# Weight loads on GpSimd's queue, and GpSimd's arithmetic shared out between ScalarE and VectorE, in a two-layer hybrid trunk

## The chip, the cores and the metric

The kernel runs on one core of one Trainium2 chip. The metric is the device time of one execution in microseconds (us), from the first to the last instruction of that core with what the device adds around them; lower is better.

## What is computed

The reference is a two-layer trunk over 768 tokens: 256 context tokens and 512 latent ones, 1024 channels each, all in float32. Each layer is a token-mixing part and a convolutional feed-forward part, both between RMS norms whose result is scaled and shifted by values made from a conditioning vector:

```python
hl = modulate(rmsnorm(xl, norm_g[l, 0]), sh1_l, sc1_l)        # the same for the context, hc
z  = split_columns(hl @ p['w_in'])                             # 6912 columns
ya = s5_branch(...)                 # diagonal state-space scan, both directions, then a GLU
yb = latent_window_attention(...)   # rotary, window of 128, sink logits
yc = hgrn2_branch(...)              # chunked gated linear recurrence, both directions
xl = xl + g1_l * rmsnorm(merge_branches(ya, yb, yc, gates, w_branch, w_out), norm_g[l, 1])
hl = modulate(rmsnorm(xl, norm_g[l, 2]), sh2_l, sc2_l)
xl = xl + g2_l * rmsnorm((silu(a) * g) @ w_down, norm_g[l, 3])  # a, g = conv(hl @ w_up)
```

The second layer does not make the context stream any further, and the latent stream is the output.

## The kernel before

**Products.** Every large product (`w_in`, `w_branch`, `w_glu`, `w_out`, `w_up`, `w_down`) runs on TensorE in a rounded 32-bit format, with each operand split into a high part and a low rest, so that a block of 128 input channels takes three matmuls: high times high, high times rest, rest times high. `wload` (line 286) brings one weight tile of 128x1024 (512 KB) into `wr`, of which there are three buffers. ScalarE writes its high part `wh`, VectorE the rest `wl = wr - wh`; with that subtraction the `wr` buffer is free, and the next load into it may start. `hold` (line 335) does the same for the down projection. The activations are split in the same way: in a norm (`norm_part`, line 552) TensorE transposes a normalized block into PSUM (`pa`), ScalarE writes h from it with scale and shift, GpSimd copies h into the rounded format (hh, the high part), and VectorE subtracts: hl = h - hh. A norm group is eight such blocks.

**Queues.** Every transfer, the 288 weight loads included, is issued by SyncE (SP), which works through its instructions in order: a load that waits for its buffer holds up all that stands behind it. GpSimd issues none. It computes the hh of the norms, the product with the sine in the rotary step (`att_in`, line 1026), the factor k of the recurrence (`hg_in`, line 1259), a few zero fills (lines 1682 and 1805), and the row of factors `mz` that a scan of the state-space branch runs with (from line 1789).

**Order.** A scheduler sets each engine's order from the program, priorities and its own estimate of durations; weight loads and their splitting have a raised priority. Work of other stages is woven in as filler: `mods_rows` (line 418) makes the modulation values of later stages with multiply-and-sum operations on VectorE (`mscr`, `macc`), on rows loaded from `in_wmodt`, and these stand between the operations of the recurrence.

**Names.** Nearly all rows carry line 121, a helper that records each operation, so one goes by the tiles: `slot` is any of 52 general SBUF buffers, `mm` and `mc` are PSUM tiles of products (512 and 256 tokens), `pa` and `pb` PSUM tiles for the rest, `yd` and `gd` branch results and gates kept in DRAM, `kd`, `tod` and `mt` tables of the state-space branch that are prepared in DRAM, `u` packed inputs of that branch in `ud`.

Of the kernel before, what the change touches and what calls it, by code (L numbers as in the profile page):

```python
# [12 lines left out]
ALU = mybir.AluOpType  # L13
# [113 lines left out]
class Trunk:  # L127
# [158 lines left out]
    def wload(self, src, n=1024):  # L286

        nc = self.nc
        raw = self.t(self.wp, [P, 1024], "wr", F32, bufs=WR)
        wh = self.t(self.wp, [P, 1024], "wh", F32R, bufs=WHB)  # L290
        wl = self.t(self.wp, [P, 1024], "wl", F32R, bufs=WHB)
        with self.tc.high_priority(offset=self.whp):
            nc.sync.dma_start(raw[:, :n], src)
            nc.scalar.activation(wh[:, :n], raw[:, :n], AF.Copy)
            with ExitStack() as ctx:
                if self.gate is not None:
                    ctx.enter_context(self.tc.issue_after(self.gate))
                nc.vector.tensor_sub(wl[:, :n], raw[:, :n], wh[:, :n].bitcast(F32))
        return wh, wl
# [35 lines left out]
    def hold(self, srcs, n):  # L335
# [3 lines left out]
        for m, src in enumerate(srcs):  # L339
# [4 lines left out]
            with self.tc.high_priority(offset=self.whp):  # L344
                nc.sync.dma_start(raw[:, :P * n], src)
                a = n * m
                while a < n * (m + 1):
                    i = a // 6
                    b = min(6 * i + 6, n * (m + 1))
                    r = raw[:, P * (a - n * m):P * (b - n * m)]  # L350
                    c = slice(P * (a - 6 * i), P * (b - 6 * i))
                    nc.scalar.activation(hi[i][:, c], r, AF.Copy)
                    nc.vector.tensor_sub(lo[i][:, c], r, hi[i][:, c].bitcast(F32))
                    a = b
# [197 lines left out]
    def norm_part(self, l, which, xr, tiles, ks, hs):  # L552
# [8 lines left out]
        for k0 in range(0, len(ks), per):  # L561
# [5 lines left out]
            for i, k in enumerate(ks[k0:k0 + per]):  # L567
                if k not in hs:
                    hs[k] = (self.s3(F32R), self.s3(F32R))
                hh, hl = hs[k]  # L570
                h = self.s3()
                nc.scalar.activation(h[:, tk], pt[:, n * i:n * i + n], AF.Identity,
                                     bias=self.mod[l][:, 8 * sh + k, tt:tt + 1],
                                     scale=self.amod[l][:, j, k, tt:tt + 1])
                nc.gpsimd.tensor_scalar(hh[:, tk], h[:, tk], 1.0, 0.0, ALU.mult, ALU.add)
                nc.vector.tensor_sub(hl[:, tk], h[:, tk], hh[:, tk].bitcast(F32))
# [441 lines left out]
    def att_in(self, l, h, t0, out):  # L1018
# [7 lines left out]
        def rope(ps, a):  # L1026
# [3 lines left out]
            nc.vector.stream_shuffle(s[:, 256:], z[:, 256:], swap)  # L1030
            nc.gpsimd.tensor_mul(s[:, 256:], s[:, 256:], sin)
            nc.vector.tensor_mul(z[:, 256:], z[:, 256:], cos)
# [198 lines left out]
    def hg_in(self, l, h, hh, t0, out):  # L1231
# [21 lines left out]
        for d, mt in enumerate((mf, mb)):  # L1253
# [4 lines left out]
            k, qf, f = self.s3(), self.s3(), self.w3()  # L1258
            nc.gpsimd.tensor_scalar(k, th, self.hgn[:, c:c + 1], self.hgc[:, c:c + 1], ALU.mult, ALU.add)
            nc.vector.tensor_scalar(f, th, self.hgb[:, c:c + 1], self.hga[:, c:c + 1], ALU.mult, ALU.add)  # L1260
# [394 lines left out]
    def s5_prep(self, l, space, per, slot):  # L1655
# [6 lines left out]
        for o in range(4):  # L1662
# [18 lines left out]
            b3 = bb.rearrange("p (d k) -> p d k", d=2)  # L1681
            nc.gpsimd.memset(bb, 0.0)
            nc.sync.dma_start(b3[:, :, 0:128], bd[:, :, 128 * o:128 * o + 128])
# [31 lines left out]
    def s5(self, l, ud, t0, res):  # L1715
# [41 lines left out]
        def stage_a(o, d, u2, la):  # L1757
# [33 lines left out]
            m3 = mz.rearrange("p (q c) -> p q c", c=96)  # L1791
            nc.gpsimd.memset(mz, 1.0)
            nc.gpsimd.tensor_mul(m3, m3, m8k[:, x0:x0 + 4].unsqueeze(2).to_broadcast([P, 4, 96]))
            nc.gpsimd.memset(m3[:, :, 0:1], 0.0)
            v.tensor_tensor_scan(xr, mz, za, 0.0, ALU.mult, ALU.add)
# [8 lines left out]
            st = 0 if d == 0 else 31  # L1804
            nc.gpsimd.memset(hcat.rearrange("p (g c) -> p g c", c=96)[:, :, st:st + 1], 0.0)
            for g2 in range(2):
# [225 lines left out]
```

## Time and profile before

| | us |
|---|---|
| median of three runs | 2694.89 (2693.42 to 2697.78) |
| the profiled execution, device time | 2701.07 |
| its span, first to last instruction | 2699.3 |
| TensorE busy | 2536.5 (94% of the span) |
| TensorE weight loads, beside the matmuls | 2129.6 (79%) |
| VectorE busy | 1896.8 (70%) |
| ScalarE busy | 1021.7 (38%) |
| GpSimd busy | 121.0 (4%) |

Row forms used below: a timeline row gives start, duration, engine (SPq is SyncE issuing transfers), operation, output and inputs, count, and in brackets how long the engine was idle before it and what ended that. A windows row gives a stretch, its length, the busy time of PE, PEld, DVE, ACT and POOL with instruction counts, the share of TensorE's full clock that was granted, the DMA share and GB/s. A granted clock near 0.5 is the lower of TensorE's two levels, 1.2 GHz; near 1.0 it is 2.4 GHz.

### The profile page before, as it was taken

How to read it: one execution, taken by the hardware profiler on the slowest of the kernel's cores; microseconds unless marked ns; L12 is line 12 of the kernel's file. 1: busy time of each engine (PE TensorE's matmuls, PEld its weight loads, DVE VectorE, ACT ScalarE, POOL GpSimd, SP SyncE). 2: the span in 40 equal slices, each digit the busy share in tenths (PEclk: the TensorE clock that was granted, in tenths of full speed). 3: DMA queues.
4: the chain of work that ended last, by engine and by line, in shares of the span. 5: the costliest groups of instructions: out<-in, count | busy, mean ns of one | idle time of the engine just before them, and what ended most of it. 6: DMA issues, size and time to landing. Idle time of an engine off the chain costs nothing. (4 is left out here: it accounts for less than half of the span.)

```text
span 2699.3 us, 47069 instructions
## 1 busy us (share of the span) xinstructions
PE 2536.5 (94%) x18436; PEld 2129.6 (79%) x18436; DVE 1896.8 (70%) x4304; ACT 1021.7 (38%) x1813; POOL 121.0 (4%) x182
## 2 busy tenths in 40 slices
PE   5999998899989999999999989899999989999998
PEld 3876776687878898887888878667787778888887
DVE  6799483778576659999974566754767856666656
ACT  3356522221223345442433463562222334443334
POOL 1100000001000010000000011000000000100000
PEclk8999999999989999999999999999999989999999
DMA  7443545453566344534434557422334565333332
GB/s 246 129 127 118 166 146 164 156 165 99 169 210 213 119 128 145 162 108 131 123 102 123 155 180 222 130 82 93 107 116 131 170 213 167 110 121 112 96 100 96
DMA packets 243214, 381.36 MB, mean 141 GB/s; under 512 B 54032, under 2 KB 139440, under 8 KB 242992
## 3 DMA queue, kind: packets, MB, share of 16 engines
q1 hardware_dynamic: 242992, 378.36, 44.8%
q8 instruction: 145, 2.38, 0.4%
q14 instruction: 77, 0.63, 0.1%
HBM read 301.26 MB, written 81.21 MB: 142 GB/s over the span
## 5 line engine op out<-in xcount | busy, mean ns | idle before, releaser
L121 PE MATMUL mm<-slot,wh 128*128 128x512 f32 (+1 forms) x3798 | 1200.3, 394 | 23.5 <-DVE slot L121 9.4
L121 PEld LDWEIGHTS mm<-slot,wh 128*128 128x128 f32 x3798 | 699.8, 190 | 160.9 <-DVE slot L121 13.4
L121 PE MATMUL mm<-slot,wl 128*128 128x512 f32 (+1 forms) x1899 | 742.3, 391 | 2.7 <-issue 1.9
L121 DVE TENSOR_TENSOR slot<-slot,slot 128x384 f32<-128x384 f32 (+17 forms) x1340 | 666.3, 535 | 101.5 <-ACT slot L121 59.3
L121 PE MATMUL mc<-slot,wh 128*128 128x256 f32 (+1 forms) x3082 | 666.7, 309 | 9.4 <-ACT slot L121 7.3
L121 PEld LDWEIGHTS mc<-slot,wh 128*128 128x128 f32 x3082 | 518.8, 193 | 57.2 <-ACT slot L121 10.8
L121 DVE TENSOR_TENSOR wl<-wr,wh 128x1024 fp32r<-128x1024 f32 (+1 forms) x274 | 333.8, 1219 | 239.3 <-ACT wh L121 235.1
L121 ACT ACTIVATE wh<-wr 128x1024 fp32r<-128x1024 f32 (+1 forms) x274 | 288.5, 1053 | 531.3 <-PE mc L121 373.0
L121 PE MATMUL mc<-slot,wl 128*128 128x256 f32 (+1 forms) x1541 | 474.6, 308 | 0.0
L121 PEld LDWEIGHTS mm<-slot,wl 128*128 128x128 f32 x1899 | 359.9, 190 | 72.8 <-DVE wl L121 1.6
L121 PEld LDWEIGHTS pa<-slot,slot 128*32 128x32 f32 (+2 forms) x5696 | 213.2, 133 | 126.5 <-issue 62.3
L121 PE MATMUL pa<-slot,slot 128*32 128x32 f32 (+8 forms) x5696 | 254.8, 227 | 57.8 <-DVE slot L121 26.5
L121 PEld LDWEIGHTS mc<-slot,wl 128*128 128x128 f32 x1541 | 296.7, 193 | 14.1 <-issue 1.2
L121 ACT ACTIVATE slot<-slot 128x768 fp32r<-128x768 f32 (+5 forms) x253 | 168.3, 669 | 367.8 <-DVE slot L121 307.7
L121 ACT ACTIVATE slot<-mm 128x512 f32<-128x512 f32 (+1 forms) x180 | 103.6, 576 | 320.7 <-PE mm L121 299.5
L121 DVE CUSTOM_DVE_ANT_0 mscr<-slot,slot 128x768 bf16<-128x768 f32 (+1 forms) x256 | 178.2, 696 | 41.0 <-DMA slot<-in_wmodt 37.5
L121 ACT ACTIVATE slot<-pa 128x512 f32<-128x512 f32 (+7 forms) x250 | 115.3, 493 | 231.0 <-PE pa L121 189.8
L121 PE MATMUL pa<-cst,slot 128*128 128x128 f32 x900 | 139.5, 286 | 23.8 <-DVE slot L121 13.2
L121 PEld LDWEIGHTS pa<-cst,slot 128*128 128x128 f32 x900 | 107.4, 145 | 53.2 <-ACT slot L121 23.4
L121 PE MATMUL mm<-slot,slot 128*128 128x256 f32 (+1 forms) x784 | 111.1, 319 | 17.4 <-DMA slot<-in_wmod 15.6
L121 DVE SCALAR_TENSOR_TENSOR slot<-slot,slot 128x256 f32<-128x256 f32 (+7 forms) x129 | 92.3, 722 | 41.0 <-ACT slot L121 40.3
L121 PEld LDWEIGHTS mm<-slot,slot 128*128 128x128 f32 (+1 forms) x784 | 93.1, 185 | 22.6 <-issue 17.9
(160 smaller groups left out, 1521.9 us busy)
## 6 DMA issues: line engine op xcount, KB each, us to landing
wr<-in_win SPq DMA_DIRECT2D x108, 512.0 KB
wr<-in_wup SPq DMA_DIRECT2D x88, 512.0 KB
slot<-in_wmodt SPq DMA_DIRECT2D x80, 384.0 KB
wr<-in_wdn SPq DMA_DIRECT2D x32, 512.0 KB
slot<-cad SPq DMA_DIRECT2D x48, 256.0 KB
wr<-in_wbr SPq DMA_DIRECT2D x24, 512.0 KB
slot<-in_wmodt SPq DMA_DIRECT2D x80, 128.0 KB
cad<-slot SPq DMA_DIRECT2D x64, 144.0 KB
```

Of the source, the lines that this page charges most:

```text
L121: return _f(*(x.ap if isinstance(x, Slot) else x for x in a), **{k: x.ap if isinstance(x, Slot) else x for k, x in kw.items()})
```

## The change

All 288 weight loads are issued from GpSimd's queue, everything else stays on SyncE's. GpSimd then computes nothing. In a norm ScalarE writes the high part hh straight from PSUM, and VectorE makes h from PSUM a second time (one multiply-add) and then hl, so that each of the 80 blocks has one ScalarE and two VectorE operations in place of one each on ScalarE, GpSimd and VectorE. The sine product (10), the zero fills (8 and 16) go to VectorE; the recurrence's k (16) and the row of factors (16) go to ScalarE, the latter with a small zero fill on VectorE in place of GpSimd's three operations.

```diff
 wload:
-            nc.sync.dma_start(raw[:, :n], src)
+            nc.gpsimd.dma_start(raw[:, :n], src)
 hold:
-                nc.sync.dma_start(raw[:, :P * n], src)
+                nc.gpsimd.dma_start(raw[:, :P * n], src)
 norm_part:
-                nc.scalar.activation(h[:, tk], pt[:, n * i:n * i + n], AF.Identity,
-                                     bias=self.mod[l][:, 8 * sh + k, tt:tt + 1],
-                                     scale=self.amod[l][:, j, k, tt:tt + 1])
-                nc.gpsimd.tensor_scalar(hh[:, tk], h[:, tk], 1.0, 0.0, ALU.mult, ALU.add)
+                a, b = self.amod[l][:, j, k, tt:tt + 1], self.mod[l][:, 8 * sh + k, tt:tt + 1]
+                nc.scalar.activation(hh[:, tk], pt[:, n * i:n * i + n], AF.Identity, bias=b, scale=a)
+                nc.vector.tensor_scalar(h[:, tk], pt[:, n * i:n * i + n], a, b, ALU.mult, ALU.add)
                 nc.vector.tensor_sub(hl[:, tk], h[:, tk], hh[:, tk].bitcast(F32))
 att_in:
-            nc.gpsimd.tensor_mul(s[:, 256:], s[:, 256:], sin)
+            nc.vector.tensor_mul(s[:, 256:], s[:, 256:], sin)
 hg_in:
-            nc.gpsimd.tensor_scalar(k, th, self.hgn[:, c:c + 1], self.hgc[:, c:c + 1], ALU.mult, ALU.add)
+            nc.scalar.activation(k, th, AF.Identity, bias=self.hgc[:, c:c + 1], scale=self.hgn[:, c:c + 1])
 s5_prep:
-            nc.gpsimd.memset(bb, 0.0)
+            nc.vector.memset(bb, 0.0)
 s5, stage_a:
-            nc.gpsimd.memset(mz, 1.0)
-            nc.gpsimd.tensor_mul(m3, m3, m8k[:, x0:x0 + 4].unsqueeze(2).to_broadcast([P, 4, 96]))
-            nc.gpsimd.memset(m3[:, :, 0:1], 0.0)
+            nc.scalar.activation(m3, m8k[:, x0:x0 + 4].unsqueeze(2).to_broadcast([P, 4, 96]), AF.Copy)
+            v.memset(m3[:, :, 0:1], 0.0)
-            nc.gpsimd.memset(hcat.rearrange("p (g c) -> p g c", c=96)[:, :, st:st + 1], 0.0)
+            v.memset(hcat.rearrange("p (g c) -> p g c", c=96)[:, :, st:st + 1], 0.0)
```

The order of the engines follows. **First place**, SyncE's queue in the first layer's recurrence, at the loads of `in_wmodt`. Before:

```order
L121 DMA tod_4663<-kd_4366 8x16x128 x3
L121 DMA wr_5901<-in_win 128x1024
L121 DMA tod_4663<-kd_4366 8x16x128
L121 DMA wr_6110<-in_win 128x1024
L121 DMA tod_4663<-kd_4366 8x16x128 x4
L121 DMA slot_769_4697<-in_wmodt 128x768
L121 DMA slot_771_4705<-in_wmodt 128x768
```

and after:

```order
L121 DMA slot_764_4679<-mid_1225 128x512
L121 DMA mt_4672<-slot_766_4686 128x512
L121 DMA mt_4672<-slot_768_4694 128x512
L121 DMA tod_4663<-kd_4366 8x16x128 x8
L121 DMA slot_769_4697<-in_wmodt 128x768
L121 DMA slot_771_4705<-in_wmodt 128x768
```

The two weight loads between the pieces of `tod` are gone from this queue; the rest stands as it stood.

**Second place**, SyncE's queue at the end of the first layer's state-space branch, where the last step's tables (`mt`) and the other branch's stored results (`yd`) are loaded. Before:

```order
L121 DMA yd_8432<-slot_1189_8426 16x8x96
L121 DMA wr_9046<-in_wglu 128x1024
L121 DMA yd_8432<-slot_1189_8426 16x8x96 x7
L121 DMA gd_8500<-slot_1196_8497 128x768
L121 DMA slot_1198_8502<-mt_5333 128x768
L121 DMA slot_1199_8504<-mt_5333 128x256
L121 DMA slot_1200_8506<-phd_1230 128x768
L121 DMA slot_1207_8551<-yd_1397 128x768
```

and after:

```order
L121 DMA slot_1198_8496<-mt_5333 128x768
L121 DMA yd_7965<-slot_1127_7959 16x8x96 x8
L121 DMA gd_8203<-slot_1157_8200 128x768
L121 DMA gd_8323<-slot_1174_8320 128x768
L121 DMA slot_1183_8386<-ud_853 128x768
L121 DMA slot_1184_8388<-mt_5333 128x768
L121 DMA gd_8384<-slot_1181_8381 128x768
L121 DMA slot_1199_8498<-mt_5333 128x256
L121 DMA slot_1200_8500<-phd_1230 128x768
L121 DMA slot_1207_8544<-yd_1397 128x768
```

The loads of `mt`, `phd` and `yd_1397` now stand ahead of the eight stores of `slot_1189` (the result of the branch's third step), and no weight load is among them.

**Third place**, VectorE at the same point, where the rests of the loaded `yd` tiles (`slot_1209`, `slot_1212`, ...) are made for the next product; `slot_1206` is the scan result of the branch. Before:

```order
L121 TENSOR_TENSOR slot_1206_8545<-slot_1203_8527,slot_1204_8528 64x4x95 x4
L121 TENSOR_TENSOR slot_1209_8554<-slot_1207_8551,slot_1208_8553 128x768
L121 TENSOR_TENSOR slot_1236_8675<-slot_1235_8670,slot_1200_8506 128x384
L121 TENSOR_TENSOR slot_1212_8560<-slot_1210_8557,slot_1211_8559 128x768
L121 TENSOR_TENSOR slot_1237_8676<-slot_1235_8670,slot_1200_8506 128x384
```

and after:

```order
L121 SCALAR_TENSOR_TENSOR slot_1189_8420<-slot_1188_8419,pa_8394 128x768
L121 TENSOR_TENSOR slot_1209_8547<-slot_1207_8544,slot_1208_8546 128x768
L121 TENSOR_TENSOR slot_1212_8553<-slot_1210_8550,slot_1211_8552 128x768
L121 TENSOR_TENSOR slot_1215_8559<-slot_1213_8556,slot_1214_8558 128x768
L121 TENSOR_TENSOR slot_1218_8565<-slot_1216_8562,slot_1217_8564 128x768
L121 TENSOR_TENSOR wl_8806<-wr_8804,wh_8805 128x1024
```

The four rests have moved ahead of the scan chain that ends in `slot_1206`.

## Rows read from the trace of the kernel before

**Rows 1.** Page, busy time, share of the span and instructions of each engine.

```profile
PE 2536.5 (94%) x18436; PEld 2129.6 (79%) x18436; DVE 1896.8 (70%) x4304; ACT 1021.7 (38%) x1813; POOL 121.0 (4%) x182
```

**Rows 2.** Waits of SyncE's queue: us in total, times, longest us.

```profile
SPq L121 <- DVE wl L121: 813.4, 204, 13.8
```

**Rows 3.** Timeline of the first layer's recurrence, 440 to 468 us.

```profile
441.63 1.97 SPq L121 DMA_DIRECT2D tod<-kd  x3
...
457.08 0.34 SPq L121 DMA_DIRECT2D wr<-in_win  x1
...
460.18 2.52 SPq L121 DMA_DIRECT2D slot<-in_wmodt  x5
...
463.79 0.96 DVE L121 CUSTOM_DVE_ANT_0 mscr<-slot,slot 128x768 bf16<-128x768 f32 x1 [6.74 <-DMA slot<-in_wmodt]
...
467.15 1.51 PE L121 MATMUL pa<-slot,slot 128*32 128x32 f32 x96 [8.91 <-DVE slot L121]
```

**Rows 4.** Windows: the stretches behind the stalls of groups 5 and 3.

```profile
784.20:792.00 7.80, 7.15 (x44) 6.22 (x45) 4.34 (x7) 4.03 (x8) 1.12 (x3) 0.51 1.05 387
...
467.10:478.00 10.90, 9.09 (x224) 7.10 (x225) 8.52 (x21) 2.23 (x6) 0.00 (x0) 0.51 1.03 345
```

**Rows 5.** Timeline at the end of the first state-space branch, 760 to 788 us.

```profile
762.23 1.69 SPq L121 DMA_DIRECT2D gd<-slot  x3
...
775.12 0.35 SPq L121 DMA_DIRECT2D wr<-in_wglu  x1
...
775.51 3.28 SPq L121 DMA_DIRECT2D yd<-slot  x7
...
779.38 0.96 SPq L121 DMA_DIRECT2D slot<-mt  x2
...
784.21 2.83 PE L121 MATMUL pa<-slot,slot 128*64 128x96 f32 x32 [9.93 <-DMA slot<-mt]
...
786.78 0.84 ACT L121 ACTIVATE slot<-slot 128x768 fp32r<-128x768 f32 x1 [11.58 <-DMA slot<-yd]
```

**Rows 6.** Timeline of the start: first weight loads, ScalarE's wait, first product with a rest.

```profile
35.00 1.00 SPq L121 DMA_DIRECT2D wr<-in_win  x2
...
49.22 0.63 ACT L121 ACTIVATE slot<-slot 128x512 f32<-128x512 f32 x1 [9.57 <-DVE slot L121]
...
53.06 0.80 PE L121 MATMUL mm<-slot,wl 128*128 128x512 f32 x1 [0.88 <-DVE wl L121]
```

**Rows 7.** Timeline of one norm group, second layer, 2325 to 2331 us.

```profile
2325.66 3.75 ACT L121 ACTIVATE slot<-pa,mod,amod 128x256 f32<-128x256 f32 x8 [4.93 <-PE pa L121]
2326.30 4.18 POOL L121 TENSOR_SCALAR slot<-slot 128x256 fp32r<-128x256 f32 x8 [11.89 <-ACT slot L121]
...
2327.47 3.62 DVE L121 TENSOR_TENSOR slot<-slot,slot 128x256 fp32r<-128x256 f32 x7 [0.30 <-POOL slot L121]
```

**Rows 8.** VectorE's groups by form: count, busy us, mean ns, idle before.

```profile
L121 DVE TENSOR_TENSOR slot<-slot,slot 128x576 f32<-128x576 f32 x80 | 58.1, 751 | 0.9 <-DMA mid<-slot 0.5
...
L121 DVE TENSOR_TENSOR slot<-slot,mm 128x256 f32<-128x256 f32 x40 | 16.4, 418 | 8.2 <-PE mm L121 7.9
```

**Rows 9.** Windows of the first feed-forward part and the norm ahead; its weight loads.

```profile
1000.00:1050.00 50.00, 48.18 (x310) 42.67 (x309) 45.29 (x97) 29.39 (x53) 9.16 (x16) 1.00 0.44 140
1050.00:1350.00 300.00, 293.33 (x1677) 258.37 (x1676) 296.35 (x762) 126.28 (x186) 0.00 (x0) 0.99 0.45 137
...
wr<-in_wup SPq DMA_DIRECT2D x23, 512.0 KB
...
wr<-in_wdn SPq DMA_DIRECT2D x12, 512.0 KB
```

**Rows 10.** Timeline of a rotary step, 140 to 143 us: VectorE beside GpSimd.

```profile
140.95 2.44 DVE L121 TENSOR_TENSOR slot<-slot,slot 128x576 f32<-128x576 f32 x2
141.20 1.64 POOL L121 TENSOR_TENSOR slot<-slot,slot 128x512 f32<-128x512 f32 x1 [8.44 <-DVE slot L121]
```

## The prediction

> **What bounds the kernel now.** I read the page's busy times first, then the waits of SyncE's queue, then the idle stretches of TensorE in the timeline with the row that ended each, and last the windows around those places. TensorE is busy 94% of the span [rows 1], so the kernel is bound by its matmuls, and a change that leaves the matmuls as they are (this one does) can win or lose only in the 163 us or so in which TensorE stands, and in the slow clock that follows a stand. That second part matters: behind two of the larger stalls the granted clock is 0.51, the lower level, while TensorE is busy 7.15 us of 7.80 and 9.09 us of 10.90 [rows 4]. VectorE is next with 70%, but the mean hides its stages: over 350 us, from the norm ahead of the first feed-forward part to the end of that part, it is idle 4.71 + 3.65 = 8.4 us [rows 9]. There VectorE is as tight as TensorE, and GpSimd is idle.
>
> The waits of SyncE's queue show what the queue move is about. It stands 204 times, 813.4 us in all, at a weight load whose buffer VectorE has not yet given back [rows 2]. Mostly nobody notices, as weights are fetched three tiles ahead. What matters is what lies behind such a load. Two of TensorE's largest stalls end with a transfer that did.
>
> **Part 1, the stall in the recurrence.** TensorE stood 8.91 us until 467.15, for VectorE, which itself had stood 6.74 us until 463.79 for rows of `in_wmodt` [rows 3]. Those rows were issued at 460.18, directly behind a weight load that went at 457.08 and the last of `tod`; the queue had already issued three pieces of `tod` by 441.63 + 1.97 = 443.60 [rows 3]. In the changed order the same loads stand there without the two weights. Five more pieces of `tod` at 1.97/3 = 0.66 us make 3.3 us, so `in_wmodt` can go at about 447, ten microseconds ahead of its need; its buffer's last readers are, by the order, matmuls of the table step well ahead. VectorE's order is unchanged there, so it goes on at 463.79 - 6.74 = 457.05, and TensorE gets its operand 467.15 - 463.79 = 3.36 us later, at 460.4 in place of 467.15. That is **-6.7**. Of the 9.09 busy microseconds at clock 0.51 that follow, up to 9.09 x 0.49 = 4.5 would come back at full clock, but VectorE is busy 8.52 of the same 10.90 us and many of the small matmuls wait for it [rows 4], so I take 2 of them: **-8.7**, between -6.7 and -11.2.
>
> **Part 2, the stall at the end of the state-space branch.** TensorE stood 9.93 us until 784.21, for `mt` [rows 5], which was issued at 779.38, behind a `w_glu` tile that SyncE could issue only at 775.12 and behind seven stores of 3.28 us. 2.6 us later ScalarE gets the first loaded `yd`, for which it had stood 11.58 us. After the change `mt`, `phd` and the four `yd` loads stand ahead of those stores, behind the `gd` stores that went at 762.23, and VectorE makes the rests ahead of its scan chain. All of them can land by about 772. Then the product on `yd` is ready when TensorE comes to it, and the stall closes; half of the slow clock behind it (7.15 x 0.49 = 3.5 at most [rows 4]) comes too, so **-12**. At least the weight goes away in front of the stores: 779.38 - 775.12 = 4.3, so the bounds are -4.3 and -13.4.
>
> **Part 3, the start.** The first two weight loads were issued at 35.00, behind the loads that the first modulation needs; ScalarE then stood 9.57 us until 49.22 in front of its weight rounding, and the first product with a rest ran at 53.06 [rows 6]. From a queue of their own three weights go at once. This helps the first product and takes its toll: 1.57 MB moved ahead of the modulation weights at 387 GB/s, the rate of a stretch with the engines full [rows 4], delays these by 4.1 us, and the norm with them. VectorE has more to do here as well. Bounds: -9.6 (the whole of ScalarE's wait) and +4.1. Nothing in the trace decides; I take the middle, **-3**.
>
> **Part 4, the norms.** In a norm group ScalarE needs 3.75 us, GpSimd 4.18 and VectorE 3.62 for seven of eight blocks, paced by GpSimd [rows 7]. Without GpSimd hh is there 2326.30 - 2325.66 = 0.64 us sooner. But VectorE has a second operation on each block: one that reads PSUM at this size takes 0.418 us [rows 8], with 0.52 for the subtraction 0.94 per block, 7.5 us a group in place of 4.2. Behind it on VectorE wait the next group's scaling and the next `wl`. TensorE needs the blocks one at a time, so for a single group little of the 3.3 us is seen. Three groups stand ahead of the first feed-forward part: 24 x 0.418 = 10.0 us against 8.4 us of idle time up to 1350 [rows 9]. So between nothing and all 10 there, and up to 4 for the other groups: **+5**, bounds 0 and +14.
>
> **Part 5, the rest.** The rotary sine product leaves GpSimd: two VectorE operations beside it took 2.44 us [rows 10] where two alone take 2 x 0.751 [rows 8], 0.94 saved, and at most 0.75 is paid for the product on VectorE; about nothing. 40 small fills on VectorE at no more than 0.42 each (a full 256-wide operation) are 17 us spread over an engine that idles 30%: **+1**, 0 to +2. k and the factor row go to ScalarE, busy 38% [rows 1]; its idle time covers them, and without it 32 operations of the norm's size (3.75/8 = 0.47) or double would be 15 to 30 us of ScalarE. The other 200 waits at weights hide nothing as large; **-1**, 0 to -3.
>
> **The sum.** -8.7 - 12 - 3 + 5 + 1 - 1 = -18.7 us. On the profiled execution, 2701.07, that is 2682.4. This execution lies 6.2 us above the median, so the forecast for the median is **2676**. The bounds add up to -37 and +9; that all go one way is unlikely, so this case alone reaches from 2664 to 2692.
>
> **Rivals.** (a) *VectorE pays for the issue of weights on GpSimd* (slower). Nothing in this trace shows a transfer issued by GpSimd. What it shows is that the two engines hinder each other: the pair of operations beside one of GpSimd's took 0.94 us more [rows 10]. If an issue did that to VectorE, then 23 + 12 = 35 weight loads in the stretch where it has no idle time [rows 9] cost 33 us, and the sum is -18.7 + 33 = +14: **2709**. It decides from 18.7/35 = 0.53 us per load. Against it: the loads are single instructions, and elsewhere VectorE has time. A rule of the Trainium skill speaks for such a tie and against the change: "SBUF — State Buffer", section "SBUF: two separate sides", says that descriptors of a transfer on GpSimd's queue are written by GpSimd itself, which is shut out of a port it shares with VectorE while certain VectorE operations run, and the other way round. It prices the transfer's delay, not VectorE's: about 0.6 us alone, 3.1 us beside such an operation. By that alone weights would come some 2.5 us late (an estimate from that page), which three buffers cover, and the sum would stay. No row here shows either.
>
> (b) *The freed waits are taken by the next ones* (same). In part 1 VectorE's chain, in part 2 the scan chain is as late as the transfer was, no clock is regained, and the queue move is worth nothing but the start: -3 + 5 + 1 = +3, at best with the 4.3 of part 2 -1, so **2694 to 2698**. For it: behind the stalls VectorE is busy 8.52 of 10.90 and 4.34 of 7.80 us [rows 4]. Against it: both releasing rows are transfers [rows 3, 5], and VectorE itself stood for one. The Trainium skill has a rule of this outcome too: "DMA: Bandwidth & Descriptors", section "Issuing engines are not separate DMA queues", says that all issuers share the same 16 engines and a second issuer saves only the usually small time of initiating. The trace does not agree for this kernel: 813.4 us of waiting in order, against 0.34 us to issue [rows 2, 3].
>
> (c) *Both stalls close with the clock, and the norms cost nothing*: -11.2 - 13.4 - 5 - 3 = -33, **2662**. For it: hh comes sooner in each group. Against it: no idle time on VectorE to put 10 us into.
>
> **How the numbers follow.** Forecast 0.57, (a) 0.12, (b) 0.16, (c) 0.15. A measurement of this kernel tells about 0.2% (5.4 us) from no change, that is 2689.5 and 2700.3. The forecast's upper end lies beyond the first by little (0.03 of it goes to same, 0.01 of (b) beyond the second): faster 0.69, same 0.18, slower 0.13. The range leaves out (a) and the far end of (c): 2655 to 2700.
>
> **What would show it.** Right: SyncE no longer waits for `wl`; `in_wmodt` issued near 447 and VectorE not standing for it; a recurrence stall near 2 us and none over 3 us before `mt`; granted clock near 1.0 around 780; VectorE operations between 1050 and 1350 of the same mean length; norm groups on VectorE of some 7 us. Wrong: longer `wl` subtractions or TensorE waiting for `wl` in the feed-forward part (a); a stall at the same two places that VectorE or ScalarE ends (b); the first product with a rest later than 53 us (part 3).

## The result, and the profile after

The changed kernel took 2714.06 us (median of four, 2711.15 to 2719.17) against 2696.34 for the kernel before on the same chip: ratio 1.0071, 95% interval 1.0052 to 1.0090. It is slower by some 18 us, where 2676 was predicted and 2700 was the upper end. Its profiled execution lasted 2713.32 us, with a span of 2710.9.

The page of the changed kernel, busy time and DMA queues (packets, MB, share of 16 engines):

```profile
PE 2545.0 (94%) x18436; PEld 2135.4 (79%) x18436; DVE 1909.7 (70%) x4434; ACT 1049.6 (39%) x1845; POOL 152.5 (6%) x292
...
q1 hardware_dynamic: 201520, 229.44, 26.8%
q0 software_dynamic: 40448, 148.92, 17.7%
```

Against [rows 1] the two busy engines have little more to do, TensorE +8.5 and VectorE +12.9 us; ScalarE's +27.9 fall on an engine that is busy 39%, and GpSimd's 152.5 are the issuing of 288 loads. The weights are the 148.92 MB of the second queue. Waits by queue, SyncE first, then GpSimd:

```profile
SPq L121 <- DVE slot L121: 838.2, 204, 51.7
SPq L121 <- ACT slot L121: 360.3, 81, 26.9
...
POOL wr L121 <- DVE wl L121: 2220.3, 253, 81.4
```

The wait of [rows 2] has left SyncE's queue; GpSimd now stands it out. So the change does what it says.

**Where the time went.** I laid the traces side by side by TensorE's work: every matmul form gets a fixed length (its median in the kernel before), and the times are compared at which equal sums of work are done. Each column comes from one execution. Where TensorE's own order differs, a figure moves by one or two us with the lengths taken (e13 at 810.5, e8 at 1797.9). The table gives the time in the kernel before and, for each run below, how much later (+) or earlier it is there. "Mixing" is the first layer's token mixing; `e1` and so on are the experiments.

| place (time before) | changed | e1 | e5 | e6 | e12 | e8 | e9 | e13 |
|---|---|---|---|---|---|---|---|---|
| first products (160.9) | +0.4 | -9.1 | -9.2 | -8.1 | -1.7 | -3.4 | -7.8 | -7.4 |
| before the recurrence (415.9) | +6.0 | -9.1 | -7.7 | -6.7 | -1.5 | -4.3 | -7.1 | -5.8 |
| behind part 1's stall (489.0) | -5.2 | -7.8 | -20.1 | -6.9 | -12.5 | -14.1 | -9.3 | -18.9 |
| behind part 2's stall (810.5) | -8.2 | -10.6 | -21.8 | -13.0 | -12.4 | -15.1 | -13.4 | -28.7 |
| feed-forward begins (1071.5) | -3.4 | -7.5 | -17.4 | -8.6 | -7.0 | -11.4 | -9.7 | -21.6 |
| second layer begun (1660.6) | +28.4 | +4.8 | -5.6 | +27.0 | +10.2 | +1.3 | +1.9 | -11.2 |
| in its mixing (1797.9) | +19.3 | -6.8 | -13.9 | +15.4 | -0.1 | -13.5 | -7.6 | -21.6 |
| its mixing done (2228.9) | +10.4 | -14.8 | -20.3 | +9.2 | -13.1 | -31.0 | -20.3 | -28.4 |
| second feed-forward part, near its end (2639.1) | +10.9 | -14.5 | -19.9 | +9.6 | -12.4 | -31.7 | -19.7 | -28.1 |

The profiled executions differ by 10.9 us at the end where the medians differ by 18: the one of before lay above its median. Read down the column of the changed kernel: part 1 gains 11.2, part 2 gains next to nothing, and the first feed-forward part with what follows it loses 31.8.

**Part 1** came as predicted. Timeline of the changed kernel, SyncE's queue and TensorE's operations of the recurrence, and the window behind:

```profile
439.75 5.91 SPq L121 DMA_DIRECT2D tod<-kd  x8
445.76 2.40 SPq L121 DMA_DIRECT2D slot<-in_wmodt  x5
...
462.87 1.05 PE L121 MATMUL pa<-slot,slot 128*32 128x32 f32 x96
...
467.00:478.00 11.00, 9.51 (x199) 6.55 (x199) 9.23 (x26) 2.14 (x5) 0.53 (x1) 0.84 0.48 140
```

`in_wmodt` goes at 445.76, not 460.18 [rows 3]; the 96 small matmuls, which had waited 8.91 us, wait for nothing that the row names; and the clock of that stretch is 0.84, not 0.51 [rows 4].

**Part 2** did not. The loads are early: `mt` at 753.51, `yd` from 754.51, against 779.38 and later [rows 5]. But TensorE stands at the same place for as long. Timeline of the changed kernel: SyncE, VectorE, TensorE.

```profile
753.51 0.43 SPq L121 DMA_DIRECT2D slot<-mt  x1
...
754.51 3.16 SPq L121 DMA_DIRECT2D slot<-yd  x4
...
767.90 2.90 DVE L121 TENSOR_TENSOR slot<-slot,slot 128x384 f32<-128x384 f32 x6
770.72 1.80 DVE L121 TENSOR_TENSOR_SCAN slot<-slot,slot 128x384 f32<-128x384 f32 x2
...
780.37 1.80 DVE L121 TENSOR_TENSOR_SCAN slot<-slot,slot 128x384 f32<-128x384 f32 x2
782.08 4.75 DVE L121 TENSOR_TENSOR slot<-slot,slot 128x384 f32<-128x384 f32 x12
786.87 0.69 DVE L121 SCALAR_TENSOR_TENSOR slot<-slot,mm 128x512 f32<-128x512 f32 x1
...
787.61 0.79 PE L121 MATMUL mm<-slot,wh 128*128 128x512 f32 x1 [11.96 <-DVE slot L121]
```

The product on `yd` ran early, as forecast, and was in PSUM when TensorE stopped at 775.65. Its evacuation is a single VectorE operation of 0.69 us. In VectorE's order it stands behind two scan chains, which last from 767.90 to 786.83; only then is the PSUM tile free. That is rival (b) at this place.

**The start.** GpSimd issues the first three weights at once, beside the input. Rows of the changed kernel, then of the kernel before:

```profile
1.26 1.72 POOL L121 DMA_DIRECT2D wr<-in_win  x3 [0.81 <-POOLq L2021]
...
1.66 9.89 SPq L121 DMA_DIRECT2D slot<-in_x  x12
...
18.35 3.85 PE L121 MATMUL mm<-slot,slot 128*32 128x512 f32 x8 [18.35 <-DVE rs_v L121]
```

```profile
1.65 6.25 SPq L121 DMA_DIRECT2D slot<-in_x  x12
```

Issuing the twelve input loads takes 9.89 us in place of 6.25, and the first matmul starts at 18.35 in place of 15.6. By 50 us this is made up: at 110 us the changed kernel is 4.0 us ahead of the kernel before, and falls back behind that (see part 3 below).

**The first feed-forward part.** Two places in the changed kernel. At the first, POOL and SP issue, then VectorE and TensorE:

```profile
1233.79 0.53 POOL L121 DMA_DIRECT2D wr<-in_wup  x1 [8.02 <-DVE wl L121]
...
1234.13 0.33 SPq L121 DMA_DIRECT2D mid<-slot  x1
...
1238.67 1.43 DVE L121 TENSOR_TENSOR slot<-slot,slot 128x576 f32<-128x576 f32 x2 [1.90 <-DMA mid<-slot]
...
1252.27 0.69 DVE L121 TENSOR_TENSOR slot<-slot,mm 128x512 f32<-128x512 f32 x1
...
1253.01 0.80 PE L121 MATMUL mm<-slot,wh 128*128 128x512 f32 x1 [10.24 <-DVE slot L121]
```

A weight goes the moment VectorE has freed its buffer, 0.34 us ahead of the store `mid`. The store lands at 1238.64, 4.5 us after its issue; in the kernel before the same store took 2.0 (1234.34 to 1236.34), with the weight issued behind it. VectorE must have that store's buffer back and stands 1.90 us; it has no slack here [rows 9], and TensorE stands 10.24 us for VectorE a little later, where before it had stood 4.26 for VectorE and 1.55 for ScalarE. By the comparison of the table this place costs some 4 us against the kernel before, but only 0.3 against `e1_arith`, where TensorE stops as well (2.92 us for ScalarE and 5.53 for VectorE).

The second place costs most, 9.1 us against the kernel before from 1350 to 1360 of its time. GpSimd's and SyncE's issues, VectorE, TensorE, and the window behind:

```profile
1349.33 0.53 POOL L121 DMA_DIRECT2D wr<-in_wup  x1 [7.94 <-DVE wl L121]
...
1349.79 2.10 SPq L121 DMA_DIRECT2D phd<-slot  x4
...
1354.93 0.18 DVE L121 TENSOR_TENSOR slot<-slot,slot 128x16 f32<-128x16 f32 x1 [1.91 <-DMA phd<-slot]
...
1362.51 0.80 PE L121 MATMUL mc<-slot,wh 128*128 128x256 f32 x2 [4.38 <-DVE slot L121]
...
1362.00:1368.00 6.00, 5.49 (x19) 4.91 (x20) 5.97 (x16) 1.90 (x2) 0.00 (x0) 0.50 0.20 79
```

The four stores `phd`, issued 0.46 us and more behind a weight, take 4.3 to 4.65 us. VectorE stands 1.91 us for one, TensorE then 4.38 us for VectorE, and behind that the clock is 0.50, its lower level, for 6 us.

### The profile page after: what moved, and what is told of

Same layout as the page of the kernel before. It is cut to its first block, busy times and chain, and to the rows that moved or that the text cites. A ratio compares the mean times of both kernels' runs of the same rounds, so it can differ in the third digit from the quotient of the medians.

```text
span 2710.9 us, 47090 instructions
## 1 busy us (share of the span) xinstructions
PE 2545.0 (94%) x18436; PEld 2135.4 (79%) x18436; DVE 1909.7 (70%) x4434; ACT 1049.6 (39%) x1845; POOL 152.5 (6%) x292
## 3 DMA queue, kind: packets, MB, share of 16 engines
q0 software_dynamic: 40448, 148.92, 17.7%
## 4 chain that ended last, share of the span: by engine, by line
PE 37%; DVE 13%; issue 12%; DMA 4%; ACT 2%; SPq 1%; POOL 1%; DVEq 0%; POOLq 0%; ACTq 0%
PE mm L121 21%; PE mc L121 9%; DVE slot L121 8%; PE pa L121 6%; DVE mscr L121 2%; ACT slot L121 2%; DVE wl L121 2%; DMA slot<-in_wmodt 1%; PE pb L121 1%; SPq L121 1%; POOL wr L121 1%; DMA wr<-in_win 1%; DVE rs_u L121 0%; DMA wr<-in_wdn 0%; DMA cad<-slot 0%
## 5 line engine op out<-in xcount | busy, mean ns | idle before, releaser
L121 DVE TENSOR_TENSOR slot<-slot,slot 128x384 f32<-128x384 f32 (+14 forms) x1350 | 654.3, 521 | 102.5 <-ACT slot L121 62.4
L121 PE MATMUL pa<-slot,slot 128*32 128x32 f32 (+8 forms) x5696 | 254.2, 227 | 34.0 <-ACT slot L121 11.6
L121 PE MATMUL mm<-slot,slot 128*128 128x256 f32 (+1 forms) x784 | 113.2, 330 | 20.3 <-DVE rs_v L121 18.4
L121 POOL DMA_DIRECT2D wr<-in_win x108 | 57.1, 529 | 1217.4 <-DVE wl L121 989.5
L121 DVE SCALAR_TENSOR_TENSOR slot<-slot,slot 128x256 f32<-128x256 f32 (+7 forms) x129 | 92.4, 724 | 39.1 <-ACT slot L121 38.7
```

The source lines that it names most:

```text
L121: return _f(*(x.ap if isinstance(x, Slot) else x for x in a), **{k: x.ap if isinstance(x, Slot) else x for k, x in kw.items()})
```

## The experiments

The theories after the result (the forecasts below call Q theory C where transfers are meant). **Q**: the second queue costs; weights that no longer keep their place in SyncE's order travel beside the stores and loads that VectorE and TensorE wait for. **V**: the extra VectorE operations cost. **O**: only the scheduler's new order costs.

### The two halves of the change, and two of its parts

`e1_arith` leaves the weights on SyncE's queue; `e3_queue` is the other half, the kernel before with the two changed lines.

```diff
-            nc.gpsimd.dma_start(raw[:, :n], src)
+            nc.sync.dma_start(raw[:, :n], src)
```

> The arithmetic of the change alone: weight loads back on SyncE's queue, the rest as changed. Theory V (VectorE pays: 80 more operations in the norms, some 45 us of VectorE, 10 us of it ahead of a feed-forward part where VectorE has 8 us to spare): this kernel is slower than before by the 17 us that the change lost in the first feed-forward part, without the 11 us that the queue gained in the recurrence, so about 2710 to 2720. Theory Q (the queue pays: weights that go the instant their buffer is free run beside the small stores and loads that VectorE and TensorE wait for): this kernel is as fast as before, 2692 to 2700, and VectorE no longer waits for the stores of mid and cad in the feed-forward part.

> The queue alone: weight loads on GpSimd's queue, all arithmetic as before, so that GpSimd's operations stand in one row with weight loads that wait for their buffers. If the loads hold up the operations (the reason to empty GpSimd), a norm group waits for a weight buffer, a whole product of 5 to 9 us each time, in ten groups and 16 scans: 2720 to 2800. If the order keeps clear of that: theory V says the queue's 11 us are gained and nothing lost, about 2682; theory Q says as slow as the changed kernel, about 2712.

`e1_arith`: 2687.49 us, ratio 0.9960 (0.9945 to 0.9974), faster. `e3_queue`: 2707.97, 1.0035 (1.0022 to 1.0048), slower. So the arithmetic is a gain and the queue a loss; V falls. `e1_arith` came out faster than either theory had said: Q had expected no gain from the arithmetic. `e2_act_twice` replaces the norm's VectorE operation by a second one of ScalarE, and `e4_first_sp` leaves the first three weights on SyncE's queue:

```diff
-                nc.vector.tensor_scalar(h[:, tk], pt[:, n * i:n * i + n], a, b, ALU.mult, ALU.add)
+                nc.scalar.activation(h[:, tk], pt[:, n * i:n * i + n], AF.Identity, bias=b, scale=a)
```

```diff
-            nc.gpsimd.dma_start(raw[:, :n], src)
+            self.wn = getattr(self, "wn", 0) + 1
+            (nc.sync if self.wn <= 3 else nc.gpsimd).dma_start(raw[:, :n], src)
```

> The changed kernel, with the second copy of the norm's h made by ScalarE (a second activation from PSUM) in place of VectorE. Theory V: the 17 us of the first feed-forward part come back and the gain of the recurrence stays, about 2695 or below. Theory Q: nothing comes back, 2710 to 2718, since ScalarE has time and VectorE was not what decided. ScalarE then needs 16 operations of 0.47 us per norm group, 7.5 us, which could cost 0 to 3 us per group on its own.

> The changed kernel with its first three weight loads on SyncE's queue, where they stand as before behind the loads of the modulation. If these three, running ahead of the modulation weights, cost at the start (the first matmul came 2.8 us later), the first matmul is back at 15.6 us and the whole is 2 to 4 us faster, about 2711. If what was lost up to 300 us (12 us from 50 to 300) comes from VectorE's added work or from transfers, 2713 to 2716.

`e2_act_twice`: 2711.42, 1.0044 (1.0028 to 1.0060); 80 operations fewer on VectorE and little gained. In the first feed-forward part it loses 21.9 us in place of 31.8, but 8.6 of that difference is gone by 1797.9. `e4_first_sp`: 2707.29, 1.0028 (1.0015 to 1.0041); the first matmul is back at 15.3 us, and the whole is 7 us faster than the changed kernel, more than forecast. It is not the early start itself that pays: at 110 us the two are within 0.2 us of each other, and the gain comes between there and 416 us.

### The queue in one stretch at a time

A flag sends the weights to GpSimd's queue in one stretch alone, with the arithmetic as changed: `e5_only_mid` from the first layer's recurrence to the end of its state-space branch, `e6_only_ffn` in the two feed-forward parts, `e12_not_ffn` everywhere but there and at the first three weights.

```diff
+        self.wq = True        # around self.ffn(l, t0) in e6; around hgrn and s5 of layer 0 in e5
...
-            nc.gpsimd.dma_start(raw[:, :n], src)
+            (nc.gpsimd if self.wq else nc.sync).dma_start(raw[:, :n], src)
```

> All arithmetic as changed; weights on GpSimd's queue only from the first layer's recurrence to the end of its state-space branch (gates' columns of w_in, w_branch of two branches, w_glu), on SyncE's queue everywhere else. If the queue move gains only where SyncE stood in front of in_wmodt and loses elsewhere, this keeps the 15 us that the arithmetic alone gained and adds the 12 us gained between 416 and 489 us: about 2675. If a queue of their own costs wherever it is used, the gain of the place is eaten within the branch: 2684 to 2690.

> All arithmetic as changed; weights on GpSimd's queue only in the two feed-forward parts. VectorE's and TensorE's orders are those of the arithmetic alone (e1) but for a few rows. Theory C (two queues: a transfer that starts beside a weight lands later than in one queue, and a chain of them is waited for): the loss that the changed kernel has against e1 around the end of the first feed-forward part comes back, 10 to 18 us, so 2697 to 2706. Theory O (the scheduler's order, which is another one with the queue of its own, is what costs): as e1, 2685 to 2691.

> The complement of e6_only_ffn: the changed kernel, but the weights of both feed-forward parts and the first three weights go by SyncE's queue. Theory of the two queues, with the loss sitting in the first feed-forward part and at the start: the 20 us that e6_only_ffn lost against e1_arith come back from e4_first_sp (2707.3), about 2685 to 2690, and the stretch from 1071 to 1660 us shows nothing against e1_arith. Rival (the loss comes from the order that follows once anything is issued elsewhere, or sits elsewhere too): 2697 or more.

`e5_only_mid`: 2680.67, 0.9940 (0.9924 to 0.9957), faster than both kernels and between its two forecasts; from 415.9 to 489.0 it gains 12.4. `e6_only_ffn`: 2707.74, 1.0041 (1.0026 to 1.0056), 20 us above `e1_arith`. `e12_not_ffn`: 2689.49, 0.9971 (0.9961 to 0.9981), 18 us below `e4_first_sp`. Together the last two place the main loss in the feed-forward parts, and by the table in the first one and just behind it: `e6_only_ffn` loses 35.6 us from 1071.5 to 1660.6 and `e1_arith` 12.3, while in the second, from 2339.5 on, they stay together. From 1071.5 to 1660.6 `e12_not_ffn` loses 17.2, where the forecast was what `e1_arith` loses; one execution of each does not tell the 4.9 us between them from noise.

`e6_only_ffn` and `e1_arith` have nearly the same order on VectorE (some 46 of 4434 operations stand elsewhere), which speaks against O. What VectorE waits for in the first feed-forward part, `e6_only_ffn` first, then `e1_arith` (us in total, times, longest):

```profile
DVE slot L121 <- DMA mid<-slot: 4.9, 3, 1.9
DVE slot L121 <- DMA phd<-slot: 2.2, 2, 1.7
DVE slot L121 <- DMA cad<-slot: 2.0, 4, 0.7
```

```profile
DVE slot L121 <- DMA mid<-slot: 2.0, 3, 1.2
...
DVE slot L121 <- DMA phd<-slot: 0.3, 1, 0.3
```

Store waits rise from 2.3 to 9.1 us on an engine without slack. TensorE falls behind at five places: 1.6 us at 1238 (4.8 lost, 3.2 of them gained just before), 8.6 at 1350, then 4.1, 3.9 and about 5 around three stops for loads of `cad`.

At 1350 `e1_arith` shows that the weight need not have overtaken anything. There too the four stores `phd` are issued behind a weight, 0.73 us behind it and in the same queue, but they take 3.55 to 3.9 us where they take 4.2 to 4.5 in `e6_only_ffn`. VectorE stands 0.27 us, TensorE 0.15, and the clock stays at 1.00; in `e6_only_ffn` they stand 1.73 and 4.13 us, and the clock falls to 0.50.

The first stop for `cad`, TensorE and the windows around it, `e6_only_ffn`, then `e1_arith`:

```profile
1449.19 1.08 PE L121 MATMUL pa<-slot,slot 128*32 128x128 f32 x16 [2.90 <-DMA slot<-cad]
...
1446.00:1452.00 6.00, 3.10 (x30) 1.73 (x28) 1.09 (x3) 0.82 (x3) 0.00 (x0) 0.73 0.63 155
1452.00:1457.00 5.00, 5.00 (x28) 4.02 (x28) 2.06 (x4) 1.92 (x3) 0.09 (x1) 0.65 0.35 101
```

```profile
1438.09 0.64 PE L121 MATMUL pa<-slot,slot 128*32 128x128 f32 x16 [1.38 <-DMA slot<-cad]
...
1436.00:1442.00 6.00, 4.55 (x49) 2.87 (x49) 2.34 (x5) 1.93 (x5) 0.00 (x0) 1.00 0.85 229
```

The stop is 1.52 us longer, and the rest of the 4.1 is the clock: in the two windows from the stop of 2.90 us on it is granted at 0.73 and 0.65, so partly at the lower level of 1.2 GHz; around the stop of 1.38 it stays at 1.00.

### Fewer bytes, in both queues

In `e8_eighth` (two queues, the changed kernel) and `e9_eighth_sp` (one queue, `e1_arith`) each weight load brings an eighth of its bytes.

```diff
-            nc.gpsimd.dma_start(raw[:, :n], src)
+            nc.gpsimd.dma_start(raw[:, :n // 8], src[:, :n // 8])   # nc.sync in e9
```

> The changed kernel, all weights on GpSimd's queue, but each load brings only an eighth of its columns (64 KB in place of 512 KB) into buffers whose rest stays zero; the output is not the reference's. The order of the engines is nearly that of the changed kernel. Theory C: with an eighth of the bytes beside them the small transfers land as if alone, VectorE's waits for stores of mid and cad (22 us) go, and the kernel takes 2685 to 2698. Theory O: the order stays and so does the time, 2706 to 2716.

> The change's arithmetic with every weight load on SyncE's queue, as in e1_arith, but each load brings only an eighth of its bytes (the rest of every weight buffer is zero), as in e8_eighth. It is the control to e8_eighth. Theory of the two queues (what costs is that weights issued by GpSimd travel beside the stores and loads of SyncE, and that in one queue they hardly do): in one queue the stretch from 1071 to 1660 us (first feed-forward part) was not paying, so fewer bytes give little there, under 4 us against e1_arith, while the stalls that SyncE's wait for weight buffers leaves (recurrence, end of the state-space branch) stay; 2675 to 2688 in all. Theory of the bytes alone (any weight traffic beside other transfers costs, whichever queue): the gain over e1_arith is like that of e8_eighth over the changed kernel, some 40 us: about 2645 to 2655.

`e8_eighth`: 2670.80, 0.9905 (0.9888 to 0.9921), 43 us below the changed kernel, and below the range that theory C had. `e9_eighth_sp`: 2686.40, 0.9961 (0.9949 to 0.9973), 1 us from `e1_arith`. In one queue the bytes of the weights cost next to nothing; in two, leaving most of them out is worth 43 us, and without them the second queue is a gain, as I had forecast for all of them. From 1071.5 to 1660.6 `e8_eighth` loses 12.7, `e9_eighth_sp` 11.6 and `e1_arith` 12.3, the changed kernel 31.8. That is Q, and leaves little of O there: between `e8_eighth` and the changed kernel some 220 of VectorE's operations stand elsewhere. `e9_eighth_sp` is the weaker control, as some 700 do between it and `e1_arith`. The stores `phd` at 1350 take 2.3 to 2.6 us in `e8_eighth`. Averages over the stretch hide the loss: its sixteen stores `mid` take 3.05 us in the changed kernel and 2.82 in `e1_arith`. A few late transfers decide, those that a saturated engine stands for.

### The transfers by themselves

`m1_pairs` and `m2_weight_first` only move data: eight times each a 256 KB store and a 384 KB load with no weight, behind a 512 KB weight in the same queue, or beside one that GpSimd or ScalarE issues. In `m2_weight_first` the store is issued 0.7 us after GpSimd's weight, in `m1_pairs` 0.3 us before it. The distances differ between the queues: in `m2_weight_first` the store comes 1.0 us after SyncE's own weight and after ScalarE's, in `m1_pairs` 0.4 and 0.

```diff
+                nc.gpsimd.dma_start(raw, w[n % 4])      # sync, scalar or none in the other modes
                 nc.sync.dma_start(mid, s[:, 0:512])
                 nc.sync.dma_start(ld, w[(n + 1) % 4][:, 0:768])
```

> The transfers alone, nothing else of the kernel: eight times each a 256 KB store and then a 384 KB load on SyncE's queue, with no weight, with a 512 KB weight ahead of them in the same queue, with one issued by GpSimd at the same moment, and with one issued by ScalarE. Theory C: store and load land later beside a weight of another queue than behind one in the same queue, the store 1 us or more (2.2 us alone, some 3 in one queue, 3.5 to 4.5 beside), and GpSimd's and ScalarE's queue do the same. Theory O: the same within 0.3 us, as all of them share the same engines.

> Transfers alone, as m1_pairs, with one multiply-free VectorE operation of 128x768 more between the write that the weight waits for and the store, so that the GpSimd-issued (or ScalarE-issued) weight starts ahead of the store as in the feed-forward part of the changed kernel. It computes nothing of the reference. Two queues side by side: the 256 KB store beside a GpSimd-issued weight takes 3.5 us or more (alone 2.2; in the changed kernel 4.5 at 1234), and the 512 KB weight stays near 5 us; if which comes first doesn't matter, the store stays at 2.0 as in m1_pairs. Behind a weight in its own queue it then takes under the 4.0 of m1_pairs, since it is issued later.

DMA issues of `m2_weight_first` (KB each, median us from issue to landing), and one row of `m1_pairs`:

```profile
wrsame<-in_wup SPq DMA_DIRECT2D x8, 512.0 KB, 3.7
wrpool<-in_wup POOLq DMA_DIRECT2D x8, 512.0 KB, 4.2
...
midnone<-snone SPq DMA_DIRECT2D x8, 256.0 KB, 2.2
midsame<-ssame SPq DMA_DIRECT2D x8, 256.0 KB, 3.4
midpool<-spool SPq DMA_DIRECT2D x8, 256.0 KB, 4.2
midact<-sact SPq DMA_DIRECT2D x8, 256.0 KB, 3.3
```

```profile
midpool<-spool SPq DMA_DIRECT2D x8, 256.0 KB, 2.0
```

The forecast for `m1_pairs`, 3.5 to 4.5 us beside GpSimd's weight, missed: 2.0. A store 0.7 us behind GpSimd's weight lands 4.2 us after its issue, ahead of it 2.0. Behind a weight in its own queue it takes 3.4 (1.0 us behind) and 4.0 (0.4 us behind), so one queue does not spare the store that stands behind a weight; what it keeps is the order where the program lists the store first. The load that follows takes 4.0 and 4.5 us there, and 4.7 and 5.1 beside GpSimd's weight. The weight from GpSimd's queue is slower too, 4.2 and 5.0 us in the two runs against 3.7 and 3.8. Whether any second queue costs, or GpSimd's alone, is open: no kernel was run with its weights on ScalarE's queue, and at unlike distances the store behind ScalarE's weight (3.3 and 3.4) cannot decide it.

### The stall of part 2, and a faster kernel

`e10_mid_act` joins `e5_only_mid` and `e2_act_twice`. `e13_act_copy` is `e5_only_mid` with the evacuation of that product (layer 0, first branch merged) moved to ScalarE:

```diff
+            y = self.w3() if first and l == 0 else None
             for p, tk in self.parts(ps, t0):
+                if y is not None:
+                    nc.scalar.activation(y[:, tk], p, AF.Copy)
+                    p = y[:, tk]
                 nc.vector.scalar_tensor_tensor(z[:, tk], tg[:, tk], 1.0, p, ALU.add, ALU.mult)
```

> The best version so far (e5_only_mid: the change's arithmetic, GpSimd's queue for the weights only from the first layer's recurrence to the end of its state-space branch) with h made by ScalarE from PSUM a second time in place of VectorE, as in e2_act_twice. If the extra VectorE operations of the norms cost what e2_act_twice gave back (2711.4 against 2714.1, -2.7), it comes to about 2678; if that difference was only the order that the scheduler found, it is 2681 give or take 4.

> The best version so far (e5_only_mid), in which ScalarE, idle there, copies the product of the first branch to be merged (layer 0, eight blocks of 128x768) out of PSUM into a buffer, and VectorE's multiply-add reads that copy: the PSUM tiles come free without waiting for VectorE's turn. If the 11.96 us stall ahead of the second product at the end of the first state-space branch is VectorE's queue (two scan chains standing ahead of one 0.69 us evacuation), it falls under 4 us, the stretch from 743 to 811 us of the kernel before is some 8 us shorter than in e5_only_mid, and the time comes to about 2673. If the products after it need something of the scan chains anyway, the stall reappears within the next few us under another name, and the time stays at 2681 give or take 4.

`e10_mid_act`: 2684.12, 0.9951 (0.9935 to 0.9967), no better than `e5_only_mid`. `e13_act_copy`: 2676.50, 0.9923 (0.9910 to 0.9937), the fastest of those that compute the whole reference, though its interval overlaps that of `e5_only_mid`. Its timeline, ScalarE, TensorE and VectorE:

```profile
767.60 0.60 ACT L121 ACTIVATE slot<-mm 128x512 f32<-128x512 f32 x1 [0.98 <-PE mm L121]
...
768.25 0.73 PE L121 MATMUL mm<-slot,wh 128*128 128x512 f32 x2 [0.69 <-ACT slot L121]
...
775.53 1.03 DVE L121 SCALAR_TENSOR_TENSOR slot<-slot,slot 128x512 f32<-128x512 f32 x2
```

TensorE stands 0.69 us in place of 11.96, while VectorE's own multiply-adds come at 775.53, no earlier than in `e5_only_mid` (773.60, in an execution 2.2 us ahead there). From 742.6 to 810.5 of the kernel before this version gains 10.4 us, `e5_only_mid` 1.3. So the stall was VectorE's order and nothing that TensorE needed of the scans. By 864.4, 4.0 of the 10.4 are given back (1.3 in `e5_only_mid`), in stops of up to 1.6 us for ScalarE, which now has the copies to make. Against `e5_only_mid` 4.2 us remain there; at the end the profiled executions differ by 8.2 and the medians by 4.2.

## Why the prediction was wrong, point by point

- **Part 1, -8.7: right.** 11.2 us in the changed kernel (12.4 in `e5_only_mid`), at the -11.2 end: much of the clock came back with the stall. Of the stretches in the table, this is the one where the queue pays.
- **Part 2, -12: wrong, and the step is "then the product on `yd` is ready when TensorE comes to it, and the stall closes".** The product was ready; its PSUM was not freed. I followed the loads and the rests but not the next operation on VectorE, the evacuation, though the printed order has the scan chain beside it. Measured from 742.6 to 810.5: -1.0. Rival (b), "what is late next", held at this place. `e13_act_copy` shows that the stall could be had, and that 4 of its 10.4 us come back soon after.
- **Part 3, -3: wrong by what it left out.** I priced the first product (it came 2.2 us sooner, at 50.82) and modulation weights delayed by up to 4.1. The input itself came late, and the first matmul by 2.8, but that is made up. Against `e1_arith` the changed kernel is 0.6 us ahead at 110 us, 9.5 behind at 160.9 and 15.1 behind at 415.9. The loss begins with a wait of VectorE for a store:

```profile
100.13 4.26 DVE L121 TENSOR_TENSOR slot<-slot,slot 128x512 f32<-128x512 f32 x6 [6.31 <-DMA cad<-slot]
```

  In `e1_arith` VectorE waits for no store between 50 and 165 us. Behind this one ScalarE stands 6.03 us for VectorE, and TensorE 2.87 us for ScalarE at 112.52; at 157.69 TensorE stands 5.66 us for ScalarE, `e1_arith` 1.79. `e4_first_sp` recovers about half (-1.8 at 415.9), though VectorE stands 8.5 us for a `cad` store in it. Why it does, and where the rest goes up to 416 us, I did not settle. The sign that I had named for this part, the first product with a rest, said right while the part lost.
- **Parts 4 and 5, +6 less 1: wrong sign.** `e1_arith` holds these two parts alone and ends 14.5 us earlier than the kernel before. By 160.9 it is 9.1 ahead: its stop for ScalarE there is 1.79 us where the kernel before has 6.66. The stretch with the norm ahead of the feed-forward part costs 3.1 and the part 12.3 more, above the 10 that I allowed there, but 11.6 of it is given back by 1797.9, and the rest of the second layer's mixing gains 8. There TensorE's waits for VectorE fall from 4.5 to 0.9 us (1660 to 1800, where the clock rises from 0.95 to 1.00) and from 9.5 to 5.6 (1800 to 2230). One cause I missed is that GpSimd's work had been slowing VectorE. VectorE's groups by form, before, then after (count, busy us, mean ns):

```profile
L121 DVE TENSOR_TENSOR slot<-slot,slot 128x256 fp32r<-128x256 f32 x72 | 35.4, 540 | 11.9 <-POOL slot L121 11.9
```

```profile
L121 DVE TENSOR_SCALAR slot<-pa,amod,mod 128x256 f32<-128x256 f32 x72 | 38.2, 542 | 8.8 <-ACT slot L121 7.8 <-PE mm L121 0.9
...
L121 DVE TENSOR_TENSOR slot<-slot,slot 128x256 fp32r<-128x256 f32 x72 | 29.6, 422 | 0.5
```

  The subtraction beside GpSimd took 540 ns and takes 422 without it (541 in `e3_queue`, where GpSimd still computes, and 418 in `e1_arith`). The new operation takes 542, where I had put 418. VectorE no longer stands 11.9 us for GpSimd, but it stands 8.8 in front of the new operation and 0.5 in front of the subtraction. So 5.8 us of work and 2.6 of standing come back for 38.2 spent: this explains a part, and why VectorE's other 30 us cost TensorE nothing in the second layer I did not settle. The Trainium skill, "SBUF — State Buffer", section "SBUF: two separate sides", has a rule on this: VectorE and GpSimd share a port that one of them holds for a whole instruction. The 118 ns agree with it. I had drawn on it for the rival alone.
- **What the sum had no term for** is the loss itself, and the step is "The other 200 waits at weights hide nothing as large", priced at -1. It was read in one direction only: I had counted what a load waits for behind a weight, and not what the others wait for when the weight travels beside them. Measured, the first feed-forward part loses 31.8 us from 1071.5 to 1660.6, against 12.3 with the weights on SyncE's queue, so 19.5 for the second queue. TensorE stands 39.1 us in it in place of `e1_arith`'s 27.5; the rest is its clock, 0.964 in place of 0.980. Over the whole, the changed kernel against `e1_arith`, the queue loses 15.1 us before the recurrence, gains 12.5 in it and loses these 19.5, and ends 25.4 behind (26.6 by the medians).
- **Rival (a) had the sign and nearly the time (2709) by a wrong mechanism.** VectorE's `wl` subtractions take 1224 ns against 1227 before, TensorE does not wait for `wl`, and the 288 issues take GpSimd 0.53 us each, 0.67 at most, though VectorE is 70% busy beside them. The late transfers that the Trainium skill's page warns of in the same section are not seen in this trace: the `w_up` loads that GpSimd issues land 3.8 us after their issue (median of 88), with VectorE busy 298.24 of 310 us in the first feed-forward part, and 4.2 and 5.0 in the two runs of transfers alone.
- The signs that I named told the cases apart: right for part 1, "a stall at the same two places that VectorE ends" for one place of (b). No sign covered stores that land later.

The other rule that I had weighed, the Trainium skill, "DMA: Bandwidth & Descriptors", section "Issuing engines are not separate DMA queues", says that all issuers' transfers run on the same 16 engines and interleave, and that a second issuer saves only the time of initiating. I set it aside because of the 813.4 us of waiting in order. The first half agrees with the case: with the weights' bytes the second queue costs, with an eighth of them it gains. The second half is too narrow here, since at one place the queue gave 12.4 us.

## What to carry to other kernels

A wait in a queue is also an order. Before moving large transfers to a queue of their own, list for each stretch what they will now overtake or travel beside, above all stores whose buffers a saturated engine needs back, and move them only where something on the critical path stands behind them (here one stretch of some 70 us). And when a stall's releaser is removed, follow the operand through to the end: the next instruction in the releasing engine's own order, evacuations of PSUM included, must be free to run.

## What the runs showed of the hardware

- A 256 KB store takes 2.2 us alone and 4.2 issued 0.7 us behind a 512 KB load of GpSimd's queue; 1.0 us behind one of ScalarE's it takes 3.3, and behind one in its own queue 3.4. A weight takes 4.2 to 5.0 us from GpSimd's queue beside these transfers and 3.7 to 3.8 from SyncE's.
- In the one-queue kernel seven eighths of the weights' bytes, some 130 MB, could be left out for 1 us of 2687, in an order that is not quite the same.
- Issuing from GpSimd took 0.53 us, steady beside a busy VectorE; GpSimd's arithmetic made a VectorE subtraction of 128x256 28% longer.
- Behind a stop of TensorE of 2.90 us the granted clock was 0.73 and 0.65, behind one of 1.38 us 1.00, so that the longer stop cost 4.1 us and not 1.5. Behind one of 4.38 us it was 0.50 for 6 us.
